# AdaLoRA forward on one core: the last row of every partition leaves in eight small stores

## The chip, the cores and the metric

The kernel runs on one NeuronCore of one Trainium2 chip. The metric is device time in microseconds (us) of one execution; the three runs shown took 166.13, 166.21 and 166.36 us, median 166.21. One further execution was profiled. The core has five engines that run their own instruction streams (PE for matrix products, DVE for vector work, ACT for copies, POOL, and SP, which here only issues transfers and waits) and sixteen DMA engines that move data between the large memory (HBM) and the on-chip memory of 128 partitions. One DMA instruction is cut into pieces for several DMA engines, and each of these adds its part to the semaphore of the transfer when its piece has landed; the semaphore stands at 16 when all has landed.

## The reference

`x` has 16 x 2048 rows of 256 floats, `W` is 256 x 256, the rank is 16.

```
x_flat = x.reshape(-1, in_dim)
y = x_flat @ W
lora_out = x_flat @ lora_A
lora_out = lora_out * lora_E
lora_out = lora_out @ lora_B
y = y + scale * lora_out
return y.reshape(batch, seq_len, out_dim).astype(np.float32)
```

33.55 MB of `x` come in and 33.55 MB of `y` go out, all in float32.

## The kernel before

The kernel first folds the low-rank part into one weight matrix, `weff = W + A * E * B * scale` (lines 190 to 199 on PE, 126 to 138 on DVE), so that what remains is one product of 32,768 rows with a 256 x 256 matrix.

The rows are cut into nine chunks by `PLAN` (line 10): 16, seven times 32, and 16 rows for each of the 128 partitions. A chunk of 32 rows is 4 MB, one of 16 rows is 2 MB. In HBM, partition p of a chunk owns `b` rows that lie one behind the other (`rows_of`, line 88), so one partition's share is one run of 32 KB, or of 16 KB in the first and the last chunk. On the chip a chunk lies in one of six buffers `xy` (line 52), and the result is written over the input in place: the buffer that a chunk was loaded into is the buffer that it is stored from.

Compute goes in steps of four rows of each partition (`Q`, line 17; 64 steps in all). In each step DVE rounds the input to bfloat16 (line 146), PE transposes it (line 176), DVE copies the transposed tile out of the accumulator memory (line 155), PE multiplies it with `weff` (line 184), and ACT copies the product back over the input in `xy` (line 163). After the last step of a chunk ACT drains and raises `s_rdy` (line 165).

All large transfers are issued by SP on one queue, in an order that is written out by hand (lines 104 to 115). SP issues the load of `W` and of the first six chunks. Then, for each chunk i, it waits until `s_rdy` says that the chunk is computed (line 108) and issues its store (line 109). After chunk 2 it also issues the loads of chunks 6, 7 and 8, each behind a wait for the store that empties its buffer (lines 110 to 113). The stores of chunks 0, 1 and 2 have semaphores of their own; the last six stores share `s_out[again]`. The last store, of chunk 8, is issued behind all others, and nothing is issued after it.

At the end SP waits for the three early semaphores (line 115, met long before), passes a barrier with the other engines, and in a second critical section waits until `s_out[again]` stands at 96, six stores of 16 each (line 213; the profile shows the instructions of that section under L243, the line where the tile context ends). Then comes a closing exchange between the engines, with a clearing of semaphores on POOL, and the program ends.

Of the kernel before, what the change touches and what calls it, by code (L numbers as in the profile page):

```python
# [9 lines left out]
PLAN = [16] + [32] * 7 + [16]  # L10

ROWS, SLOTS = 32, 6

LEAD = 6
AFTER = {2: [6, 7, 8]}

Q = 4

# [2 lines left out]
def kernel(  # L21
# [10 lines left out]
    nc = tc.nc  # L32
    P = 128
# [4 lines left out]
    out_flat = out.flatten_outer_dims()  # L38
# [4 lines left out]
    CHUNKS = len(PLAN)  # L43
    assert K == M and sum(PLAN) * P == N and all(b % Q == 0 for b in PLAN)

    def sbuf(name, shape, dt):
        return ctx.enter_context(nc.sbuf_tensor(name, shape, dt))
# [4 lines left out]
    xy = [sbuf(f"xy{s}", [P, ROWS, K], FP32) for s in range(SLOTS)]  # L52
# [17 lines left out]
    sem = tc.alloc_semaphore  # L70
# [2 lines left out]

    again = CHUNKS - SLOTS
    s_out = [sem(f"s_out{i}") for i in range(again + 1)]
    s_id = sem("s_id")
    s_lora = sem("s_lora")
    s_lpe = sem("s_lpe")
# [9 lines left out]
    def rows_of(flat, i):  # L88
        b, r0 = PLAN[i], starts[i]
        return flat[r0:r0 + b * P, :].rearrange("(p b) k -> p b k", b=b)  # L90
# [6 lines left out]
    with tc.tile_critical(sync_engine=mybir.EngineType.SP, no_gpsimd_drain=True):  # L97
        sp, pe, dve, act, pool = nc.sync, nc.tensor, nc.vector, nc.scalar, nc.gpsimd


        def load(i):
            sp.dma_start(out=xy[i % SLOTS][:, :PLAN[i], :], in_=rows_of(x_flat, i)).then_inc(s_in[i], 16)
# [3 lines left out]
            load(i)  # L106
        for i in range(CHUNKS):
            sp.wait_ge(s_rdy, i + 1)
            sp.dma_start(out=rows_of(out_flat, i), in_=xy[i % SLOTS][:, :PLAN[i], :]).then_inc(s_out[min(i, again)], 16)
            for later in AFTER.get(i, []):  # L110
                if later >= SLOTS:
                    sp.wait_ge(s_out[later - SLOTS], 16)
                load(later)
        for i in range(len(s_out) - 1):
# [6 lines left out]
            out=ident[:], in_=ident[:], compare_op=mybir.AluOpType.not_equal, fill=1.0,  # L121
# [11 lines left out]
            out=ate[:], in0=ps_at[:R, :, :], scalar1=e_sb[:], scalar2=float(scale),  # L133
# [63 lines left out]
        for c in range(KC):  # L197
            m = pe.matmul(ps_aeb[:, c, :], ate[:, c, :], b_bf[:], start=True, stop=True)  # L198
# [12 lines left out]

    with tc.tile_critical(sync_engine=mybir.EngineType.SP, no_gpsimd_drain=True):
        nc.sync.wait_ge(s_out[again], 16 * (CHUNKS - again))

# [1 line left out]
_INS = ['x', 'W', 'lora_A', 'lora_B', 'lora_E', 'scale']  # L216
# [31 lines left out]
```

## Time and profile before

| | |
|---|---|
| three runs, median | 166.21 us (166.13 to 166.36) |
| the profiled execution's own time | 165.19 us |
| its span, first to last instruction | 163.4 us |
| busy: PE / DVE / ACT | 90.8 / 84.1 / 66.1 us (56% / 51% / 40%) |
| moved by the 16 DMA engines | 67.43 MB, 413 GB/s over the span |
| DMA share by the page's row of 40 slices | 0.9 or more in all but the first and the last slice and two of 0.8 |

The span is what the instruction records cover; the profiled execution's own time is 1.79 us longer, for what lies ahead of the first and behind the last record. The median of the runs is 1.02 us above the profiled execution. Busy times are sums over an engine's instructions; PE, DVE and ACT work side by side, and none of them is busy for much more than half of the span.

Three kinds of answers are used below. The page gives shares of the whole span in 40 slices of 4.085 us. A table of windows gives, for any stretch, the busy time of each engine, the granted clock of PE, the share of the DMA engines that were moving data, and what they moved in GB/s; a packet is counted where it begins. Third, the trace holds a record of every DMA packet with its start, duration and size. These records carry no number of the DMA engine, but a packet that begins within some ns of the end of another belongs to the same engine, and so sixteen chains can be followed from 6.5 us to the end.

### The profile page before, as it was taken

The numbers are of one execution on the slowest core, as the hardware profiler recorded it, in microseconds if no ns is written. First come the engines' busy times: TensorE is split into PE (matmuls) and PEld (weight loads), VectorE is DVE, ScalarE is ACT, GpSimd is POOL, SyncE is SP. The second block draws the span as 40 slices with busy tenths as digits, with TensorE's granted clock in tenths as the row PEclk, the third lists the DMA queues.
The fourth block names the chain that finished last, engine by engine and source line by source line (L and its number), as shares of the span: only waits on it lengthen the run. The fifth ranks groups of instructions, "written<-read, shape, count | busy, mean of one in ns | idle before, by whom it ended". The sixth has DMA issues, their size and how long they took to land. (4 is left out here: it accounts for less than half of the span.)

```text
span 163.4 us, 2684 instructions
## 1 busy us (share of the span) xinstructions
PE 90.8 (56%) x1028; PEld 81.6 (50%) x1028; DVE 84.1 (51%) x132; ACT 66.1 (40%) x65; POOL 0.7 (0%) x6
## 2 busy tenths in 40 slices
PE   0169499999999999990000099999992000000000
PEld 0047389999999999980000089999981000000000
DVE  0165299999999999950000169999970000000000
ACT  3002447777777777772000026777774000000000
POOL 1000000000000000000000000000000000000000
PEclk9999999999999999999555559999999755555555
DMA  4999999899999999999999998999999999999990
GB/s 133 421 433 489 393 449 449 385 473 425 403 481 393 385 409 481 393 457 425 433 433 425 441 441 383 465 437 425 425 435 433 441 409 465 417 425 441 409 409 32
DMA packets 3203, 67.43 MB, mean 413 GB/s; under 512 B 624, under 2 KB 896, under 8 KB 896
## 3 DMA queue, kind: packets, MB, share of 16 engines
q1 hardware_dynamic: 2864, 67.37, 96.4%
q10 hardware_dynamic: 336, 0.03, 0.3%
q14 instruction: 3, 0.02, 0.0%
HBM read 33.85 MB, written 33.55 MB: 412 GB/s over the span
## 5 line engine op out<-in xcount | busy, mean ns | idle before, releaser
L163 ACT COPY xy<-ps_y 128x1024 f32<-128x1024 f32 x64 | 64.8, 1013 | 56.2 <-PE ps_y L184 56.2
L184 PE MATMUL ps_y<-weff,xt 128*128 128x256 bf16 x512 | 68.6, 278 | 0.5 <-PEq L170 0.3
L146 DVE CAST xb<-xy 128x1024 bf16<-128x1024 f32 x64 | 43.6, 683 | 24.9 <-DMA xy<-in_x_dram 24.9
L176 PE MATMUL ps_xt<-ident_bf,xb 128*128 128x128 bf16 x512 | 40.9, 226 | 24.7 <-PEq L170 24.7
L184 PEld LDWEIGHTS ps_y<-weff,xt 128*128 128x128 bf16 x512 | 48.4, 100 | 6.4 <-issue 1.1
L176 PEld LDWEIGHTS ps_xt<-ident_bf,xb 128*128 128x128 bf16 x512 | 35.5, 102 | 27.3 <-issue 25.7
L155 DVE COPY xt<-ps_xt 128x1024 bf16<-128x1024 bf16 x64 | 44.2, 691 | 5.4 <-PE ps_xt L176 3.7
L194 PE MATMUL ps_at<-ident,a_sb 128*16 128x128 f32 x2 | 0.6, 402 | 4.1 <-DMA a_sb<-in_lora_A_dram 4.1
L198 PE MATMUL ps_aeb<-b_bf,ate 16*128 16x256 bf16 x2 | 0.6, 404 | 3.6 <-DVE ate L132 3.6
L129 DVE CAST b_bf<-b_sb 16x256 bf16<-16x256 f32 x1 | 0.3, 280 | 3.9 <-DMA b_sb<-in_lora_B_dram 3.9
L163 ACT ACT_TABLE_LOAD x1 | 1.3, 1283 | 2.5 <-issue 2.5
L198 PEld LDWEIGHTS ps_aeb<-b_bf,ate 16*128 16x128 bf16 x2 | 0.1, 106 | 4.1 <-DVE ate L132 4.1
L194 PEld LDWEIGHTS ps_at<-ident,a_sb 128*16 128x16 f32 x2 | 0.1, 94 | 4.1 <-DMA a_sb<-in_lora_A_dram 4.1
L132 DVE TENSOR_SCALAR ate<-ps_at,e_sb 16x256 bf16<-16x256 f32 x1 | 0.5, 472 | 1.6 <-DMA e_sb<-in_lora_E_dram 1.6
L127 DVE CAST ident_bf<-ident 128x128 bf16<-128x128 f32 x1 | 0.2, 227 | 1.7 <-POOL ident L120 1.7
L138 DVE TENSOR_TENSOR weff<-w_sb,ps_aeb 128x512 bf16<-128x512 f32 x1 | 0.7, 687 | 0.8 <-PE ps_aeb L198 0.8
L120 POOL TENSOR_SCALAR_AFFINE_SELECT ident<-ident 128x128 f32<-128x128 f32 x1 | 0.3, 293 | 0.2 <-POOL ident L118 0.2
L118 POOL MEMSET ident<- 128x128 f32 x1 | 0.2, 204 | 0.5 <-SPq L97 0.5
L229 POOL MEMSET const-bfloat16-1.0<- 128x1 bf16 x1 | 0.1, 101 | 0.0
L229 POOL MEMSET const-uint8-127<- 128x1 uint8 x1 | 0.1, 101 | 0.0
L229 POOL MEMSET const-float32-0.0<- 128x1 f32 x1 | 0.1, 98 | 0.2 <-issue 0.2
L229 POOL MEMSET const-float32-1.0<- 128x1 f32 x1 | 0.1, 98 | 0.0
## 6 DMA issues: line engine op xcount, KB each, us to landing
xy<-in_x_dram SPq DMA_DIRECT2D x7, 4096.0 KB, 29.1
out_dram<-xy SPq DMA_DIRECT2D x7, 4096.0 KB, 39.5
xy<-in_x_dram SPq DMA_DIRECT2D x2, 2048.0 KB, 16.3
out_dram<-xy SPq DMA_DIRECT2D x2, 2048.0 KB, 39.3
w_sb<-in_W_dram SPq DMA_DIRECT2D x1, 256.0 KB, 2.9
a_sb<-in_lora_A_dram ACTq DMA_DIRECT2D x1, 16.0 KB, 3.1
b_sb<-in_lora_B_dram ACTq DMA_DIRECT2D x1, 16.0 KB, 4.4
e_sb<-in_lora_E_dram ACTq DMA_DIRECT2D x1, 0.1 KB, 5.7
```

Source lines behind the costliest of these rows:

```text
L120: pool.affine_select(out=ident[:], in_=ident[:], compare_op=mybir.AluOpType.not_equal, fill=1.0, base=0, pattern=[[-1, P]], channel_multip ...
L129: dve.tensor_copy(out=b_bf[:], in_=b_sb[:]).then_inc(s_lora, 1)
L132: dve.tensor_scalar(out=ate[:], in0=ps_at[:R, :, :], scalar1=e_sb[:], scalar2=float(scale), op0=mybir.AluOpType.mult, op1=mybir.AluOpType. ...
L138: dve.tensor_add(out=weff[:], in0=w_sb[:], in1=ps_aeb[:]).then_inc(s_lora, 1)
L146: dve.tensor_copy(out=xb[k % 2][:], in_=xy[i % SLOTS][:, r:r + Q, :]).then_inc(s_xb, 1)
L155: dve.tensor_copy(out=xt[k % 2][:], in_=ps_xt[k % 2][:]).then_inc(s_xt, 1)
L163: act.copy(out=xy[i % SLOTS][:, r:r + Q, :], in_=ps_y[k % 2][:]).then_inc(s_y, 1)
L176: t = pe.transpose(ps_xt[k % 2][:, j, c, :], xb[k % 2][:, j, c * P:(c + 1) * P], ident_bf[:])
L184: m = pe.matmul(ps_y[k % 2][:, j, :], xt[k % 2][:, j, c, :], weff[:, c, :], start=(c == 0), stop=(c == KC - 1),)
L194: t = pe.transpose(ps_at[:R, c, :], a_sb[:, c, :], ident[:])
L198: m = pe.matmul(ps_aeb[:, c, :], ate[:, c, :], b_bf[:], start=True, stop=True)
L229: nc = _bacc.Bacc("TRN2", target_bir_lowering=False, num_devices=1)
```

## The change

The last store, of chunk 8, now takes the first 15 of the 16 rows of each partition. The sixteenth row of each partition, 1 KB, goes out in eight further stores over consecutive groups of 72, 15, 14, 12, 8, 4, 2 and 1 partitions (together 128), which are issued behind it on the same queue. These stores run over 12, 15, 14, 12, 8, 4, 2 and 1 DMA engines. Each has a semaphore of its own, and the last critical section waits for all eight after the wait for `s_out[again]`.

```
+PARTS = [72, 15, 14, 12, 8, 4, 2, 1]
...
+    s_part = [sem(f"s_part{m}") for m in range(len(PARTS))]
...
         for i in range(CHUNKS):
             sp.wait_ge(s_rdy, i + 1)
-            sp.dma_start(out=rows_of(out_flat, i), in_=xy[i % SLOTS][:, :PLAN[i], :]).then_inc(s_out[min(i, again)], 16)
+            y = xy[i % SLOTS][:, :PLAN[i], :]
+            if i < CHUNKS - 1:
+                sp.dma_start(out=rows_of(out_flat, i), in_=y).then_inc(s_out[min(i, again)], 16)
+            else:
+
+                r = PLAN[i] - 1
+                sp.dma_start(out=rows_of(out_flat, i)[:, :r, :], in_=y[:, :r, :]).then_inc(s_out[again], 16)
+                p = 0
+                for m, n_p in enumerate(PARTS):
+                    sp.dma_start(
+                        out=rows_of(out_flat, i)[p:p + n_p, r:, :], in_=y[p:p + n_p, r:, :],
+                    ).then_inc(s_part[m], 16)
+                    p += n_p
+                assert p == P
...
     with tc.tile_critical(sync_engine=mybir.EngineType.SP, no_gpsimd_drain=True):
         nc.sync.wait_ge(s_out[again], 16 * (CHUNKS - again))
+        for s in s_part:
+            nc.sync.wait_ge(s, 16)
```

What is computed, and all bytes that go to HBM, stay the same.

## The prediction

> **What bounds the kernel now.** I read the page's slices first, then SP's own waits, then windows over the last 44 us, then the packet records for what the windows leave open.
>
> ```profile
> span 163.4 us, 2684 instructions
> ...
> ACT  3002447777777777772000026777774000000000
> ...
> DMA  4999999899999999999999998999999999999990
> ...
> q1 hardware_dynamic: 2864, 67.37, 96.4%
> ...
> q14 instruction: 3, 0.02, 0.0%
> ```
>
> A digit is a tenth of a slice of 4.085 us. ACT, the last engine of each compute step, is idle from slice 31 on, that is for the last quarter of the span, while the DMA row stays at 9 until the last slice. The kernel is a transfer of 67.4 MB over 16 engines that are hardly ever idle; compute is hidden.
>
> ```profile
> engine line waited for: us in total, times, longest us
> SPq L109 <- ACTq L165: 77.6, 7, 18.4
> ...
> SPq L243 <- DMA out_dram<-xy: 36.2, 1, 36.2
> ```
>
> This is SP's queue: who waited, for whom, how long. The last wait is the one that counts: SP sits for 36.2 us at the end for the stores (its record runs from 125.98 to 162.14 us). What remains behind it is 1.27 us of closing exchange.
>
> ```profile
> 120.00:125.00 5.00, 3.52 (x38) 2.76 (x35) 1.69 (x3) 3.94 (x4) 0.00 (x0) 1.00 1.00 433
> ...
> 159.00:159.50 0.50, 0.00 (x0) 0.00 (x0) 0.00 (x0) 0.00 (x0) 0.00 (x0) 0.50 0.62 262
> 159.50:160.00 0.50, 0.00 (x0) 0.00 (x0) 0.00 (x0) 0.00 (x0) 0.00 (x0) 0.50 0.16 66
> 160.00:160.50 0.50, 0.00 (x0) 0.00 (x0) 0.00 (x0) 0.00 (x0) 0.00 (x0) 0.50 0.08 33
> 160.50:161.00 0.50, 0.00 (x0) 0.00 (x0) 0.00 (x0) 0.00 (x0) 0.00 (x0) 0.50 0.08 33
> 161.00:161.50 0.50, 0.00 (x0) 0.00 (x0) 0.00 (x0) 0.00 (x0) 0.00 (x0) 0.50 0.15 66
> 161.50:162.00 0.50, 0.00 (x0) 0.00 (x0) 0.00 (x0) 0.00 (x0) 0.00 (x0) 0.50 0.00 0
> ```
>
> The last two columns are DMA share and GB/s. At full rate the sixteen move 433 GB/s. In half a us, 33 GB/s are 16.4 KB, one packet of the last store. So between 160.0 and 161.5 us only four packets begin: two engines are still at work while fourteen have finished. The chains of packets say the same with times: fourteen engines end between 159.16 and 160.09 us, two at 161.65 and 161.74 us. I call the later one X, the other Y. Their completions land 0.45 and 0.37 us after that, at 162.10 and 162.11, and SP goes on at 162.14; the third-latest landing is at 160.43. **The end is set by two DMA engines, 1.7 us behind the others**, and only what happens to their last 16 KB pieces moves it.
>
> Why they are late: on X two packets of 8 KB of the instruction queue, at 41.4 and 118.7 us (309 ns each, and the data packets behind them took 652 and 359 ns longer than the usual 1213); on Y a run of slow packets, 1311 to 1316 ns, from 117.6 us, on top of an earlier lag. Neither cause is touched by the change. Which numbers X and Y bear, no record says.
>
> **The change, part by part.** All sums are shifts of one engine's end, made in the profiled execution (span 163.4 us, own time 165.19, against a median of 166.21); I add the shift to the median.
>
> *Fifteen rows for sixteen.* Each engine has 8 partitions of the last store. Starts of back-to-back packets lie 1209.5 ns apart at 32 KB and 607 ns at 16 KB, so a KB costs (1209.5 - 607) / 16 = 37.7 ns. Eight packets shorter by 1 KB: -301 ns on every engine.
>
> *The small stores.* 1 KB packets took 46 ns in 214 of 272 records (44 in 27 more), and each starts 3 ns before its forerunner's end: 43 ns. A completion packet of 4 B takes 9, so 6. All 1 KB records are loads (`W` and `lora_B`); a 1 KB store does not occur. The bounds are 38 ns (the pure byte price) and 116 ns (the slowest in the packed stretch of these loads, first answers of 0.4 us and more left out). I take 43, since data and completion packets of stores follow one another as tightly as those of loads.
>
> How many KB an engine gets follows from the counts in the change: 72 rows over 12 engines are 6 each, all other groups 1 each. I assume that each group counts from the same end. Then the engines, in that order, get 13, 12, 11, 11, four times 10, four times 9, and the last four 2, 2, 1 and 0 KB, with 8, 7, 6, 6, 5, 4, 2, 2, 1 and 0 more completions. The shifts are: first engine 13 x 43 + 8 x 6 - 301 = +306 ns; second +257; the next two +208; four at 10 x 43 + 5 x 6 - 301 = +159; four at +110; then 2 x 43 + 2 x 6 - 301 = -203 twice, -252, and -301. If the groups did not count from one end, an engine would get about the mean of 8 KB, 8 x 43 + 4 x 6 - 301 = +67 ns.
>
> *Eight issues on SP.* A store's issue takes 332 to 431 ns in these rows, a load's up to 632; eight are 2.7 to 5.1 us, from 125.2 to at most 130.3 us. They are hidden by the 36.2 us wait; the backlog of 34 us on every engine means that the small stores stand in the queue long before their turn. Without that cover they would cost the full 2.7 to 5.1. Behind them on SP stand only the three waits of line 115 and the barrier, which move by the same time into the same wait; the other engines are done by 124.7 us.
>
> *Eight waits behind the last one.* SP's waits carry two semaphores per instruction in this trace, and unmet waits aside they stand 61 to 70 ns apart between 125.58 and 125.98 us: four instructions of 65 ns, 260 ns if all of them come after the last landing. How many do depends on which store lands last. For the fourth of the light engines (0 KB) it is the big store, so all four follow: -301 + 260 = -41 ns. For the next (1 KB) three: -252 + 195 = -57. For the two with 2 KB two: -203 + 130 = -73. For the heavy ones: four with 9 KB two, +110 + 130 = +240; four with 10 KB one, +159 + 65 = +224; two with 11 KB one, +273; +257 and +306 with none. The bound below is 0 for the waits, if met waits run out in parallel with the closing work, and above 8 x 70 = 560 ns if each is an instruction of its own.
>
> *Sum.* Whatever numbers X and Y bear, the shift is between -0.07 and +0.31 us, with the later of the two deciding. If at least one is among the twelve that get 9 to 13 KB, +0.22 to +0.31; the other fourteen have 1.6 us of room and do not matter.
>
> **A rule that speaks against the change.** The packet chains show two late engines without numbers. The Trainium skill, page "DMA: Bandwidth & Descriptors", section "Latency and other measured facts", states that engines 7 and 15 are usually slower in traces than the rest, with a guessed cause in GpSimd's descriptors, which this kernel doesn't use. The same page ("Why a DMA increments its semaphore by 16 and not by 1") states that a transfer over k engines takes the lowest-numbered k. By these two, engine 15 would lose 8 KB but engine 7 gain 2, and the end would follow engine 7: +0.22 us, an estimate of 166.43 us; no run here shows the numbers.
>
> **The rivals.**
>
> *A, my forecast: a late engine is among the heavy twelve.* By count alone, two engines out of sixteen both fall among the light four with a chance of 4 x 3 / (16 x 15) = 5%; the instruction queue is surely tied to particular engines, so I don't trust the count that far. The middle of 0.22 to 0.31, nearer to the eight engines with 9 and 10 KB: +0.24, **166.45 us**. Its own range reaches from +0.07 (nine at 38 ns, 24, less 301, free waits) to +0.95 (ten at 116, 30, less 301, a wait).
>
> *B: both X and Y are light.* Both fetches of X come from one queue, so its place is fixed in every run, and a light end would gain each time. -0.04 to -0.07: 166.15 us; -0.30 (165.91) if the waits cost nothing.
>
> *C, on the other side: completions that wait for one another.* The first engine sends nine completions in a row, and each says that what went before has landed. If each can only follow the landing of the one before (0.37 us from packet to landing above), eight cost 3.0 us: that engine, whose last landing of 159.51 to 160.43 moves by 0.31 anyway, would land its last at 162.8 to 163.7 in place of 162.11, +0.7 to +1.6. It decides from 0.17 to 0.29 us per completion (the room of 1.7 to 2.6 us, less 0.31, over 8). For it: no row has nine completions in a row. Against it: the completions of `W` and `lora_A` landed on the sixteen engines at 3.43 to 3.86 and 3.63 to 4.03 us, 0.2 apart and not 0.37, and the packet behind a completion starts at once. I price it at its cheap end, +0.7: 166.9.
>
> *D: the stores are not what they are said to be.* Were 15 rows cut into KB packets, 120 x 43 - 8 x 607 = +304 ns would stand in place of -301, and +0.24 would become +0.85: 167.05. Were a group to run on one engine, 72 x 43 = 3.1 us there: +1.2 to +2. Against: the 16 rows of the first and last chunk, in buffers of 32, went as single packets of 16 KB.
>
> *E: an instruction fetch more.* SP's program grows by about 12 instructions. The fetches of 41.4 and 118.7 us each cost an engine 0.7 to 1.0 us; one more on X or Y gives 167.2, on another engine nothing.
>
> **How the numbers follow.** A 0.45, B 0.25, C 0.15, D 0.08, E 0.07. A measurement of this kernel can tell about 0.2%, 0.33 us, from no change. A splits into 0.29 within, 0.14 slower (small stores dearer than 43 ns) and 0.02 faster; B into 0.12 faster (it lies within by the sum, but with free waits at the edge) and 0.13 within; C, D and E are slower. Together: faster 0.14, same 0.42, slower 0.44. The time is that of A, which by itself lies within 0.2%; its own range is 166.28 to 167.16, and 166.28 to 166.6 with small stores of 38 to 60 ns. The range goes from B with nearly free waits, 165.95, over C to the cheap end of D, 167.1.
>
> **What would show it.** Right: eight small issues ending by 131 us; the last store's packets of 15 KB at about 573 ns; the DMA window after 160 us as thin as before, ending 0.1 to 0.3 us later; a wait that ends 0.2 us later. B would show the end of the packets 0.2 to 0.3 us earlier and four short waits eating it. C would show packets done early and landings spread out behind them. D shows 1 KB packets by the thousand, E a fourth packet of the instruction queue. I am wrong altogether if the two late engines don't recur in the new run.

## The result and the profile after

The changed kernel takes 167.02 us (median of 12 runs, 166.58 to 167.52) against 165.88 us before (12 runs, 165.38 to 166.36): ratio 1.0072, 95% interval 1.0057 to 1.0086, which is +1.19 us (0.95 to 1.43; the two medians lie 1.14 us apart). The profiled execution took 167.31 us, with a span of 165.5 us.

The page of the changed kernel, its DMA row and its table of queues, shows a kernel that still does nothing but move data:

```profile
span 165.5 us, 2696 instructions
...
DMA  4999998989999899999999999999999999999950
...
q1 hardware_dynamic: 3060, 67.37, 95.2%
...
q14 instruction: 3, 0.02, 0.0%
```

As many bytes and as many packets of the instruction queue as before. So rival E is out (no fourth fetch), and so are the thousands of 1 KB packets of rival D: 196 more packets than before on the data queue, 128 of them the 1 KB stores.

SP's part, from the timeline of SP, from its waits and from the instructions of lines 229 and 261 (columns of the latter: count, duration in ns min/median/max, first and last start in us):

```profile
125.89 0.33 SPq L118 DMA_DIRECT2D out_dram<-xy  x1
126.27 7.56 SPq L121 DMA_DIRECT2D out_dram<-xy  x8
```

```profile
SPq L229 <- DMA out_dram<-xy: 29.3, 1, 29.3
```

```profile
L229 SPq EVENT_SEMAPHORE  x2: 28/1384/2741, 161.1 to 163.9; - x2
```

```profile
L261 SPq EVENT_SEMAPHORE  x7: 17/28/28, 163.9 to 165.5; - x7
```

The eight small issues take 7.56 us, 0.88 to 1.0 us each, where I took 0.33 to 0.63. They end at 133.8 us and are hidden. From 134.5 us on SP stands for 29.3 us. The instruction that it stands at waits for two semaphores, those of the stores over two and over four engines; its record of 2741 ns begins when the first is met (last landing 161.08 us) and ends at 163.84 us with the second. Behind it six more wait instructions run (one more of line 229, five of line 261), each already met, about 61 ns apart, to 164.24 us. The compiled order is nearly that of the text reversed: the big store is waited for last.

Windows over the tail (DMA share and GB/s in the last two columns):

```profile
159.00:159.50 0.50, 0.00 (x0) 0.00 (x0) 0.00 (x0) 0.00 (x0) 0.00 (x0) 0.50 0.76 265
159.50:160.00 0.50, 0.00 (x0) 0.00 (x0) 0.00 (x0) 0.00 (x0) 0.00 (x0) 0.50 0.11 31
160.00:160.50 0.50, 0.00 (x0) 0.00 (x0) 0.00 (x0) 0.00 (x0) 0.00 (x0) 0.50 0.15 61
...
162.00:162.50 0.50, 0.00 (x0) 0.00 (x0) 0.00 (x0) 0.00 (x0) 0.00 (x0) 0.50 0.06 18
162.50:163.00 0.50, 0.00 (x0) 0.00 (x0) 0.00 (x0) 0.00 (x0) 0.00 (x0) 0.50 0.04 12
163.00:163.50 0.50, 0.00 (x0) 0.00 (x0) 0.00 (x0) 0.00 (x0) 0.00 (x0) 0.50 0.00 0
```

The same picture as before: fourteen engines end by 160 us, two go on alone. But nothing moves after 162.8 us, while SP is released only at 163.84. Before, that gap was 0.4 us (161.74 to 162.14); now it is 1.04. The records of completions landing on the semaphores show what fills it. These are the late landings (those of X and Y), in us, by store:

```
store          completions of the two late engines
15 rows        162.278  162.672
72 partitions  162.513  162.916
15             162.701  163.096
14             162.886  163.275
12             163.071  163.452
 8             163.255  163.628
 4                      163.816
 2, 1          none late (last at 161.08 and 160.84)
```

Read down a column: behind the 72 partitions the completions of one engine land 0.18 to 0.19 us apart. In the packet records the same completions stand 48 ns apart, with one 1 KB packet between two. So landings do not keep up with completions that stand so close, and on the late engines five or six of them queue up. The landings of the eight stores number 12, 15, 14, 12, 8, 4, 2 and 1, one for each engine of the store. The table also says where the late engines are: both take part in the store over eight engines, one in that over four, none in that over two.

The loss adds up from the trace of after: -0.30 us for the fifteen rows, 163.816 - 162.672 = +1.14 us from the landing of the big store to the last landing, and 164.243 - 163.876 = +0.37 us of waits: **+1.21 us, against 1.19 measured**. The two profiled spans differ by 2.1 us, more than that: in this execution the late engines' data ended 0.85 us later than it would by the bytes. That part differs from execution to execution: in the seven kernels here that move the same bytes up to there, the completion packet of the 15-row store on the later engine begins between 161.71 and 162.40 us. The sum is therefore compared with the medians.

### The profile page after: what moved, and what is told of

The parts are those of the page before. It is cut to its first block, busy times and chain, and to the rows that moved or that the text cites. A ratio compares the mean times of both kernels' runs of the same rounds, so it can differ in the third digit from the quotient of the medians.

```text
span 165.5 us, 2696 instructions
## 1 busy us (share of the span) xinstructions
PE 92.8 (56%) x1028; PEld 82.9 (50%) x1028; DVE 84.1 (51%) x132; ACT 66.1 (40%) x65; POOL 0.7 (0%) x6
## 5 line engine op out<-in xcount | busy, mean ns | idle before, releaser
L200 PE MATMUL ps_y<-weff,xt 128*128 128x256 bf16 x512 | 69.9, 282 | 0.5 <-PEq L186 0.3
L192 PE MATMUL ps_xt<-ident_bf,xb 128*128 128x128 bf16 x512 | 41.7, 229 | 24.2 <-PEq L186 24.2
L192 PEld LDWEIGHTS ps_xt<-ident_bf,xb 128*128 128x128 bf16 x512 | 36.4, 103 | 27.0 <-issue 25.2
```

What stands on the lines that cost most here:

```text
L192: t = pe.transpose(ps_xt[k % 2][:, j, c, :], xb[k % 2][:, j, c * P:(c + 1) * P], ident_bf[:])
L200: m = pe.matmul(ps_y[k % 2][:, j, :], xt[k % 2][:, j, c, :], weff[:, c, :], start=(c == 0), stop=(c == KC - 1),)
```

## The experiments

Theory T is the one just read off: the spacing of completions on the late engines, and the waits behind it. All ratios are against runs of the kernel before on the same chip (median 165.87 to 165.90 us).

**The small stores ahead of the big one.** Same transfers, same issues, same waits; only the order in the queue differs.

```
-    sp.dma_start(out=rows_of(out_flat, i)[:, :r, :], ...).then_inc(s_out[again], 16)
     p = 0
     for m, n_p in enumerate(PARTS):
...
+    sp.dma_start(out=rows_of(out_flat, i)[:, :r, :], ...).then_inc(s_out[again], 16)
```

> The eight small stores are issued ahead of the 15-row store, in place of behind it; bytes, packets, issues and waits stay. Theory T (completions of one DMA engine land no closer than about 0.18 us apart, and on the two late engines five or six of them queue up behind the data; the waits behind the last landing add 0.37 us): the completions now land while 4.5 us of data still follow, so only the dearer KB packets remain, +0.16 to +0.21 us on an engine with 10 or 11 KB, and at most 0.1 us of waits: 0.15 to 0.3 us above the kernel before, about 0.9 to 1.0 us below the changed kernel. Rival P (the small packets and small transfers slow the engines themselves, or their long issues on SP matter): no better than the changed kernel, +0.9 to +1.2 us. Rival W (the waits alone): +0.8 or more, since all nine waits are still there.

Measured: 1.0004 (0.9992 to 1.0016), +0.07 us (-0.13 to +0.27). The loss is gone. SP's waits in this kernel:

```profile
SPq L229 <- DMA out_dram<-xy: 25.6, 1, 25.6
SPq L120 <- ACTq L181: 4.8, 1, 4.8
SPq L261 <- DMA out_dram<-xy: 3.5, 1, 3.5
```

The wait for the small stores (25.6 us) now ends at 159.25 us, before that for the big store (3.5 us more). Their completions land 0.18 to 0.20 us apart on the late engines here too, but 3.5 us of data still follow. The time is below T's 0.15 to 0.3 us, with an interval that reaches into it. Rival P falls: the packets and the eight issues are as they were, and cost nothing. Rival W is not tested by this run: the big store's wait comes last in the compiled order, so all the others are over by 159.56 us, and none stands behind the last landing any more. W's forecast did not allow for that; the next run decides on it.

**One semaphore for the eight.**

```
-    ).then_inc(s_part[m], 16)
+    ).then_inc(s_part[0], 16)
...
-        for s in s_part:
-            nc.sync.wait_ge(s, 16)
+        nc.sync.wait_ge(s_part[0], 16 * len(PARTS))
```

> The eight small stores count on one shared semaphore, with one wait for 128 in place of eight waits; the transfers are the same. T: the sixth-to-last waits fall away, six instructions of 61 ns = 0.37 us less than the changed kernel, so +0.75 to +0.9 us above before; completions still spaced by about 0.18 us in the landings. P: no change against the changed kernel, +1.1 to +1.2. W: nearly all of the loss gone, +0.2 or less.

Measured: 1.0042 (1.0027 to 1.0057), +0.70 us (0.45 to 0.95). The instructions of the last section:

```profile
L260 SPq EVENT_SEMAPHORE  x6: 17/22/30067, 133.7 to 165.2; - x6
```

The long wait of 30.07 us ends at 163.92 us, and the branch behind it begins at 164.02: 0.10 us, where the eight semaphores cost 0.40. So of the 1.19 us the waits make up about 0.3 by the trace (0.5 by the times, 1.19 less 0.70, with an interval that holds 0.3), and the larger part stays: the last packet ends at 162.86, the last landing is at 163.90. W falls here, since 0.70 us are left with almost no wait behind the last landing; P falls again.

**One store of 128 partitions for the sixteenth rows**, and **the sixteenth rows left out.**

```
-PARTS = [72, 15, 14, 12, 8, 4, 2, 1]
+PARTS = [128]
```

> The sixteenth rows go out in one store of 128 partitions (8 KB on every DMA engine) with one semaphore. T: one more completion per engine, 0.35 us of data behind the one before, so none queues: 8 x 43 + 6 - 301 = +0.05 us of packets and at most 0.13 us of waits, 0 to +0.2 us above before. P by packets (cost goes with the number of 1 KB packets, 8 here against 10 or 11 on the late engines): +0.7 to +0.9 us.

```
-    for m, n_p in enumerate(PARTS):
-        sp.dma_start(out=rows_of(out_flat, i)[p:p + n_p, r:, :], ...).then_inc(s_part[m], 16)
```

> The sixteenth row of each partition of the last chunk is not stored at all; the output lacks these 128 rows. T and all rivals: 8 KB less on every engine, -0.30 us against before. If it is 0, the end does not follow the bytes of the last store.

Measured: 1.0000 (0.9986 to 1.0014), that is 0 +- 0.23 us, for the one store; 0.9971 (0.9959 to 0.9983), -0.48 us (-0.68 to -0.28), without the rows. The first says that 1 KB packets, and the cut into 15 rows and one, cost nothing that can be measured. The second says that the end does follow the bytes on the late engines; -0.30 lies within its interval, near the edge.

**Four and eight equal stores.** Every engine gets 8 KB again, as from the one store; only the number of completions behind the data changes.

```
-PARTS = [128]
+PARTS = [32] * 4
```

```
-PARTS = [128]
+PARTS = [16] * 8
```

> As the single store of the sixteenth rows, but cut into four stores of 32 partitions with one shared semaphore: every DMA engine gets 8 KB, 2 KB from each, so bytes and packets are those of the single store and only the completions behind the data grow from one to four. T (0.185 us from landing to landing): the last landing comes 4 x 0.185 = 0.74 us behind that of the 15-row store, whose own comes 0.30 earlier than before: +0.44, with up to 0.1 of waits +0.4 to +0.55 us above before. P (packets or bytes): as the single store, 0 +- 0.2.

> The same with eight stores of 16 partitions: 8 KB on every engine, 1 KB from each, eight completions. T: 8 x 0.185 - 0.30 = +1.18, with waits +1.1 to +1.3 us above before, more than four stores by 4 x 0.185 = 0.74; all sixteen engines land their last about 1 us behind their last packet. P: 0 +- 0.2.

Measured: four stores 1.0036 (1.0016 to 1.0056), +0.60 us (0.27 to 0.93); eight stores 1.0087 (1.0069 to 1.0106), +1.44 us (1.14 to 1.76). With 0.00 for one store, seven more completions cost 1.44 us, 0.21 us each (the medians of the kernel with eight stores and of the one before lie 1.29 us apart, which is 0.18 each). The windows of the kernel with eight stores:

```profile
162.00:162.50 0.50, 0.00 (x0) 0.00 (x0) 0.00 (x0) 0.00 (x0) 0.00 (x0) 0.50 0.08 23
162.50:163.00 0.50, 0.00 (x0) 0.00 (x0) 0.00 (x0) 0.00 (x0) 0.00 (x0) 0.50 0.00 0
163.00:163.50 0.50, 0.00 (x0) 0.00 (x0) 0.00 (x0) 0.00 (x0) 0.00 (x0) 0.50 0.00 0
```

The data is out by 162.48 us, and the landings go on to 163.90: on one late engine every 0.187 to 0.189 us, on the other every 0.180 to 0.181. This is the shape of the whole effect: a stretch of more than a us with no byte moving. By this trace the cost is 163.90 - 162.455 us from the landing of the 15-row store to the last, less 0.30: 1.14 us, at the lower end of the measured interval. Whether the rest up to 1.44 is more than noise stays open.

With four stores, two 1 KB packets lie between two completions, which stand 90 to 91 ns apart in the queue, and the late landings are again 0.18 to 0.19 us apart. So the spacing goes with the number of completions and not with the packets between them. What sets it, whether a completion waits for the one before it or for the landing of the data between the two, no run here parts.

**Many stores, but on the first two engines.** As many issues and completions as before, on engines that are early.

```
-PARTS = [16] * 8
+PARTS = [112] + [2] * 8
```

> The sixteenth rows in nine stores on one shared semaphore: one of 112 partitions (7 KB on each engine) and eight of two partitions, which run on two engines. As many issues and completions as with eight stores of 16 and more, but the late two engines get one small store only. T: the two engines with nine completions land at about 161.1 to 161.8, before the late ones; 0 to +0.2 us against before. P (each small store costs something wherever it runs) or a late engine among the two: +1.2 us or more.

Measured: 0.9999 (0.9990 to 1.0008). The two engines with nine small stores land their last at 161.18 and 161.83 us, 0.17 to 0.18 us behind one another; the late ones, with one small store each, land at 162.20 and 162.46 and set the end. So it is the count on the late engines that matters, and nine stores as such are free.

**An attempt at a faster kernel, and what it ran into.** Since both late engines belong to the first eight, I tried to hand 16 KB of each of these to the other eight, through POOL.

```
+            n_p = P if i < CHUNKS - 1 else P - 16
+            sp.dma_start(out=rows_of(out_flat, i)[:n_p], in_=xy[i % SLOTS][:n_p, :PLAN[i], :], ...
...
+        for m in range(2):
+            pool.dma_start(out=turn[m][:], in_=W[8 * m:8 * m + 8, :16]).then_inc(s_turn[m], 16)
+            pool.wait_ge(s_rdy, CHUNKS)
+            p = P - 16 + 8 * m
+            pool.dma_start(out=rows_of(out_flat, last)[p:p + 8], in_=xy[last % SLOTS][p:p + 8, :PLAN[last], :], ...
```

> From the kernel before: the last store takes 112 partitions (seven of 16 KB on each engine in place of eight), and the other 16 partitions go out in two stores of eight partitions that POOL issues, each behind a small load of 8 x 64 B from W that turns POOL's choice of eight engines. Every byte of the output is still stored. If the two stores fall on the eight engines that the late two don't belong to (the landings of the changed kernel put both late ones among the first eight), each late engine is relieved of 0.61 us and the early ones, with 1.6 us of room, take 0.61 more: -0.4 to -0.6 us against before. If they fall on the late eight: +0.5 to +0.7. If POOL spreads them over all sixteen: 0 to +0.2.

Measured: 1.0392 (1.0348 to 1.0436), +6.5 us: a miss, and not one of the three cases. The records (of an execution of 173.42 us, one of the two longest of six) show 16 KB packets of up to 2.35 us in place of 0.61, while POOL's stores run (130 to 138 us) and again when the store of 112 partitions runs (from 155.8 us). To part the two, the cut by partitions alone, on SP:

```
+            cuts = [0, P] if i < CHUNKS - 1 else [0, P - 16, P]
+            for p, e in zip(cuts, cuts[1:]):
+                sp.dma_start(out=rows_of(out_flat, i)[p:e], in_=xy[i % SLOTS][p:e, :PLAN[i], :], ...
```

> From the kernel before: the last store is cut by partitions into 112 and 16 (seven and then one run of 16 KB on each engine), both issued by SP on one semaphore, with nothing on POOL. It asks what made the kernel with the side stores slow. If the split of 112 partitions makes engines read partitions that other engines are reading too, its 16 KB packets take well over 611 ns here as well, and the loss is +2 to +6 us. If it was POOL's transfers: packets of 611 ns, and 0 to +0.15 us.

Measured: 1.0156 (1.0128 to 1.0184), +2.6 us (2.1 to 3.1). Windows of this kernel:

```profile
155.00:157.00 2.00, 0.00 (x0) 0.00 (x0) 0.00 (x0) 0.00 (x0) 0.00 (x0) 0.50 1.17 418
157.00:159.00 2.00, 0.00 (x0) 0.00 (x0) 0.00 (x0) 0.00 (x0) 0.00 (x0) 0.50 0.91 352
159.00:161.00 2.00, 0.00 (x0) 0.00 (x0) 0.00 (x0) 0.00 (x0) 0.00 (x0) 0.50 0.46 164
161.00:163.00 2.00, 0.00 (x0) 0.00 (x0) 0.00 (x0) 0.00 (x0) 0.00 (x0) 0.50 0.12 49
```

Busy engines move less: a share of 1.17 for 418 GB/s, where 1.00 gave 433. Of the 128 packets of 16 KB, 18 took more than 0.65 us and the longest 2.29; before, all 128 took 611 ns. So the cut into 112 and 16 costs by itself; the remaining 4 us of the other kernel came with POOL's stores of eight partitions, which are cut differently again. That engines then read the same part of the on-chip memory is argued, not shown. The small stores of the changed kernel and of the one with nine stores were cut by partitions too, and there all 128 packets of 1 KB took 46 ns. No version that beats both kernels was found.

## Why the prediction was right, and where it was not

**What bounds the kernel.** Right. In the nine traces whose large stores are whole across the partitions the same pattern recurs: fourteen engines are done by 159.8 to 160.5 us, two end 1.2 to 2.8 us after the last of these, and the end follows those two. Where the same number of stores was put on early engines, the time did not move.

**Case A, a late engine among the heavy twelve.** Right: one late engine had 11 KB and six small stores, the other 10 KB and five. The -301 ns of the fifteen rows (573 ns packets) and the 1 KB packets of 46 ns were as taken. The upper bound of 116 ns was not the slowest of its stretch (loads at 2.8 us took 155, 226 and 233 ns), but no small store came near it.

**The step that failed.** The sum let the last landing follow the last packet by a fixed time, 0.37 to 0.45 us, whatever stood in front of it, and charged 6 ns for a completion. In the queue the 6 ns were right. But on X and Y the completions stood 48 ns apart and landed 0.18 to 0.19 apart, so that the last landing came 163.82 - 162.80 = 1.02 us behind the last packet in place of 0.37: 0.64 us that the sum of A lacks. I had this mechanism as rival C, with a threshold of 0.17 to 0.29 us for each completion, and with the row that gave its size (the completions of `W` and `lora_A`, 0.2 us apart). But I charged it to the engine with the most completions, which has the room, and not to the late engines, which have none. The first engine, with nine completions, landed at 160.84 us and did not matter. C's 0.37 us for each was twice the measured size, and its place was wrong.

**The waits.** I counted on the order of the text, with two semaphores in each instruction and so one instruction or two behind the last landing. The compiled order was nearly the reverse, and six followed: 0.37 us in place of 0.07 to 0.13. The duration, 61 ns apart, was right.

**The issues on SP.** 0.88 to 1.0 us each, where I took at most 0.63. Hidden as said; the small stores stood in the queue 25 us before their turn.

**B, D, E.** B fell with the landings of the stores over eight and four engines. D fell: the 15 rows went as packets of 15,360 B, and the landings, 12, 15, 14, 12, 8, 4, 2 and 1, show that no group ran on one engine. E fell: three instruction packets, as before.

**The rule weighed.** The Trainium skill, "DMA: Bandwidth & Descriptors", section "Why a DMA increments its semaphore by 16 and not by 1", has a transfer take the lowest-numbered engines. The landings agree in so far as the groups are nested: two late ones in the store over eight, one in that over four, none in that over two. By that rule engine 15 is not one of the late two, so its section "Latency and other measured facts", which names 7 and 15, does not fit this kernel for 15, and could for 7.

That the measured 167.02 us lies in the range of 165.95 to 167.1 is in good part luck. The upper part of the range came from C, worked out at 166.9 on an engine that did not matter, and from the cheap end of D, which fell; A's own sum gave +0.24 us, which the prediction itself could not tell from no change, and it gave "slower" 0.44 against 0.42 for "same". The single number, A's 166.45, was too low by 0.57 us: 0.64 of landings and 0.30 of waits, less what the kernel before had been measured too high by three runs (166.21 against 165.88).

## What to carry to other kernels

Before transfers are cut up to even out the DMA engines, find the engines that end last and count what each of them gets, completions too: at the very end of a queue a small transfer costs its completion, here 0.18 to 0.21 us when it runs on an engine that ends last, and not its bytes. Put small transfers ahead of the last large one, where their completions land while data still moves. And leave a large 128-partition transfer whole across partitions; here the cut along the rows (15 and 1) cost nothing, and the cut into 112 and 16 partitions cost 2.6 us.

## What the runs showed of the hardware

- Completions of one DMA engine landed 0.17 to 0.19 us apart when they stood 48 ns apart in the queue (0.180 to 0.181 on one late engine, 0.187 to 0.189 on the other, with eight in a row; 0.17 to 0.18 on the first two). The Trainium skill, "DMA: Bandwidth & Descriptors", section "Anatomy of one DMA — SWDGE (gpsimd) path", calls the semaphore write essentially free on trn2, for transfers that POOL issues. No run here times that write by itself; for stores that SP issues, completions in a row were not free.
- A small store took SP 0.75 to 1.0 us to issue directly behind another store, against 0.33 us for the 15-row store, which had waited for its data first (line 118 of the changed kernel). The place counts and not the size: with the small stores ahead, the first of them took 0.38 us and the 15-row store behind them 0.79 us.
- A last store cut into 112 and 16 partitions ran with 16 KB packets of up to 2.3 us and cost 2.6 us, though it moves the same bytes.
- The 8 KB instruction packets come in every trace at about 42, 102 and 119 us; in the trace of before, two of them fell on a late engine. In four of the other eight traces with whole large stores the packet at about 119 us can be followed without doubt, and it leads to the later of the two late engines there too. In all nine, one engine has two runs of slow 32 KB packets, 1.29 to 1.35 us in place of 1.21, at about 62 to 74 and 107 to 123 us; where they can be followed without doubt (two traces), they lead to the other late engine. What slows these packets stays open.
